# Two rows per partition, result in place, loads and stores in alternate runs: a log-softmax backward kernel on one core

## The chip, the cores and the metric

One core of a Trainium2 chip runs the kernel. The metric is the device time in microseconds (us) of one execution. The span of a profiled execution is about 2 us shorter than the reported time of the same execution. (1925.1 us below is its median when the prediction was made, 1925.3 us that with the result.)

Engines: DVE is VectorE, ACT is ScalarE, SP is SyncE (it issues all transfers here), "SPq" is SP's sequencer. "The engines" without a name are the core's 16 DMA engines, which move the data.

## The reference

```python
batch, seq_len, vocab = 8, 1024, 8192            # 8192 rows of 8192 fp32
def reference(y, dy):
    softmax_x = np.exp(y)
    sum_dy = np.sum(dy, axis=-1, keepdims=True)
    return (dy - softmax_x * sum_dy).astype(np.float32)
```

Two inputs of 268.4 MB are read and one output of 268.4 MB is written: 805.3 MB in all.

## The kernel before

A tile is 128 rows, one row (32 KiB) per partition. Per tile: load dy, load y, reduce dy on DVE, then four times exp on ACT into PSUM and one multiply-add on DVE into a half-row output tile; each finished half row is stored.

```python
    yp = ctx.enter_context(tc.tile_pool(name="yp", bufs=3))
    dyp = ctx.enter_context(tc.tile_pool(name="dyp", bufs=2))
    op = ctx.enter_context(tc.tile_pool(name="op", bufs=2))
    ...
    for i in range(n_tiles):                       # 64 tiles
        ...
        nc.sync.dma_start(out=dy_t[:], in_=dy_f[sl])
        nc.sync.dma_start(out=y_t[:], in_=y_f[sl])
        nc.vector.tensor_reduce(out=s_t[:], in_=dy_t[:], ..., negate=True)
        for h in range(n_half):                    # 2
            o_t = op.tile([P, H], fp32)
            for q in range(n_q):                   # 2
                ...
                nc.scalar.activation(e_t[:], y_t[:, cs], ...Exp)
                nc.vector.scalar_tensor_tensor(out=o_t[...], in0=e_t[:], scalar=s_t[:],
                                               in1=dy_t[:, cs], op0=mult, op1=add)
            nc.sync.dma_start(out=out_f[sl][:, h * H : (h + 1) * H], in_=o_t[:])
```

All transfers are issued by SP in one order, on one queue. That order is not quite the order of the code: the built program has it as dy0, y0, dy1, then for every tile "store, store, next y, next-but-one dy":

```
1 L50 DMACopy dy_t<-in_dy_dram 128x8192
2 L51 DMACopy y_t<-in_y_dram 128x8192
3 L50 DMACopy dy_t<-in_dy_dram 128x8192
4 L78 DMACopy out_dram<-o_t 128x4096 x2
5 L51 DMACopy y_t<-in_y_dram 128x8192
6 L50 DMACopy dy_t<-in_dy_dram 128x8192
7 L78 DMACopy out_dram<-o_t 128x4096 x2
```

## Time and profile before

| | before |
|---|---|
| time, median | 1925.1 us (1923.6 to 1926.8) |
| bytes moved | 805.3 MB at a mean of 418 GB/s |
| DMA engines' packets, share of span | 99.5% |
| DVE / ACT busy | 59% / 25% |

Lines of the page of the kernel before: span and busy time, then the DMA rows of the 40 slices (busy tenths; GB/s), the DMA queue (packets, MB, share of 16 engines), the chain that ended last, and the DMA issues (count, KB each, median us from issue to landing).

```profile
span 1924.6 us, 1253 instructions
DVE 1134.1 (59%) x320; ACT 477.5 (25%) x257; POOL 0.2 (0%) x4
...
DMA  9999999999999999999999999999999999999997
GB/s 414 426 432 415 425 424 420 423 420 423 420 414 425 422 420 423 414 424 420 421 423 414 420 422 421 418 422 422 418 426 420 418 425 425 414 425 414 425 425 318
...
q1 hardware_dynamic: 36864, 805.32, 99.5%
...
DMA y_t<-in_y_dram 61%; DVE o_t L70 29%; ACT e_t L67 6%; SPq L78 1%; DVEq L104 0%; ACTq L67 0%; SPq L51 0%; SPq L50 0%
...
dy_t<-in_dy_dram SPq DMA_DIRECT2D x64, 4096.0 KB, 27.8
y_t<-in_y_dram SPq DMA_DIRECT2D x64, 4096.0 KB, 18.3
out_dram<-o_t SPq DMA_DIRECT2D x128, 2048.0 KB, 8.7
```

One tile in the timeline of the kernel before (start us, length us, engine, line, what, count; in brackets the idle time before and what ended it):

```profile
888.61 3.68 ACT L67 ACTIVATE e_t<-y_t 128x2048 f32<-128x2048 f32 x2 [21.56 <-DMA y_t<-in_y_dram]
890.52 9.12 DVE L70 SCALAR_TENSOR_TENSOR o_t<-e_t,s_t,dy_t 128x2048 f32<-128x2048 f32 x4 [12.28 <-ACT e_t L67]
...
895.16 4.86 SPq L78 DMA_DIRECT2D out_dram<-o_t  x2
...
900.43 0.60 SPq L51 DMA_DIRECT2D y_t<-in_y_dram  x1
901.09 1.23 SPq L50 DMA_DIRECT2D dy_t<-in_dy_dram  x1
918.38 3.68 ACT L67 ACTIVATE e_t<-y_t 128x2048 f32<-128x2048 f32 x2 [21.34 <-DMA y_t<-in_y_dram]
```

### The profile page before, as it was taken

What the parts mean: (1) busy time and instruction counts of PE and PEld (TensorE: products, weight loads), DVE (VectorE), ACT (ScalarE), POOL (GpSimd) and SP (SyncE); (2) the same over time, 40 slices, a digit from 0 to 9 for tenths busy, and PEclk for the clock granted to TensorE, in tenths of its full rate; (3) what the DMA queues carried; (4) which work ended last, traced back from release to release, by engine and by line L of the source; (5) the groups of instructions that cost most, each with busy time, mean ns of one, the idle gap of its engine ahead of it and who ended that gap; (6) DMA issues with size and microseconds to landing.
All of it is one profiled execution on the core that took longest, in us unless ns stands there. A gap on an engine that the chain in (4) does not pass through costs nothing.

```text
span 1924.6 us, 1253 instructions
## 1 busy us (share of the span) xinstructions
DVE 1134.1 (59%) x320; ACT 477.5 (25%) x257; POOL 0.2 (0%) x4
## 2 busy tenths in 40 slices
DVE  5657556465564655756657556475564655646555
ACT  1322313223132131221322313223132231321312
POOL 0000000000000000000000000000000000000000
DMA  9999999999999999999999999999999999999997
GB/s 414 426 432 415 425 424 420 423 420 423 420 414 425 422 420 423 414 424 420 421 423 414 420 422 421 418 422 422 418 426 420 418 425 425 414 425 414 425 425 318
DMA packets 36874, 805.40 MB, mean 418 GB/s; under 512 B 4096, under 2 KB 4096, under 8 KB 4096
## 3 DMA queue, kind: packets, MB, share of 16 engines
q1 hardware_dynamic: 36864, 805.32, 99.5%
q14 instruction: 10, 0.08, 0.0%
HBM read 536.87 MB, written 268.44 MB: 418 GB/s over the span
## 4 chain that ended last, share of the span: by engine, by line
DMA 61%; DVE 29%; ACT 6%; issue 2%; SPq 1%; DVEq 0%; ACTq 0%
DMA y_t<-in_y_dram 61%; DVE o_t L70 29%; ACT e_t L67 6%; SPq L78 1%; DVEq L104 0%; ACTq L67 0%; SPq L51 0%; SPq L50 0%
## 5 line engine op out<-in xcount | busy, mean ns | idle before, releaser
L70 DVE SCALAR_TENSOR_TENSOR o_t<-e_t,s_t,dy_t 128x2048 f32<-128x2048 f32 x256 | 584.1, 2344 | 770.0 <-ACT e_t L67 770.0
L67 ACT ACTIVATE e_t<-y_t 128x2048 f32<-128x2048 f32 x256 | 476.2, 1877 | 1436.2 <-DMA y_t<-in_y_dram 1372.4
L53 DVE TENSOR_REDUCE s_t<-dy_t 128x1 f32<-128x8192 f32 x64 | 555.2, 8676 | 12.9 <-DMA dy_t<-in_dy_dram 12.9
L67 ACT ACT_TABLE_LOAD x1 | 1.3, 1283 | 0.7 <-PEq L93 0.7
L93 POOL MEMSET const-bfloat16-1.0<- 128x1 bf16 x1 | 0.1, 102 | 0.0
L93 POOL MEMSET const-uint8-127<- 128x1 uint8 x1 | 0.1, 102 | 0.0
L93 POOL MEMSET const-float32-0.0<- 128x1 f32 x1 | 0.1, 99 | 0.2 <-issue 0.2
L93 POOL MEMSET const-float32-1.0<- 128x1 f32 x1 | 0.1, 99 | 0.0
## 6 DMA issues: line engine op xcount, KB each, us to landing
dy_t<-in_dy_dram SPq DMA_DIRECT2D x64, 4096.0 KB, 27.8
y_t<-in_y_dram SPq DMA_DIRECT2D x64, 4096.0 KB, 18.3
out_dram<-o_t SPq DMA_DIRECT2D x128, 2048.0 KB, 8.7
```

What stands on the lines that cost most here:

```text
L53: nc.vector.tensor_reduce(out=s_t[:], in_=dy_t[:], axis=mybir.AxisListType.X, op=mybir.AluOpType.add, negate=True,)
L67: nc.scalar.activation(e_t[:], y_t[:, cs], mybir.ActivationFunctionType.Exp)
L70: nc.vector.scalar_tensor_tensor(out=o_t[:, q * CD : (q + 1) * CD], in0=e_t[:], scalar=s_t[:], in1=dy_t[:, cs], op0=mybir.AluOpType.mult, ...
L78: nc.sync.dma_start(out=out_f[sl][:, h * H : (h + 1) * H], in_=o_t[:])
L93: nc = _bacc.Bacc("TRN2", target_bir_lowering=False, num_devices=1)
```

## The change

Intent: longer contiguous runs (two rows per partition as one 64 KiB run for dy and the output), no separate output tile (the result replaces dy), and fewer changes of direction: 32 MB loaded, then 16 MB stored, 16 times, on the one queue.

```diff
-    yp = ctx.enter_context(tc.tile_pool(name="yp", bufs=3))
-    dyp = ctx.enter_context(tc.tile_pool(name="dyp", bufs=2))
-    op = ctx.enter_context(tc.tile_pool(name="op", bufs=2))
+    R = 2
+    BATCH = 2
+    dy_v = dy.flatten_outer_dims().rearrange("(g p r) d -> g p (r d)", p=P, r=R)
     ...
+    dyp = ctx.enter_context(tc.tile_pool(name="dyp", bufs=BATCH))
+    yp = ctx.enter_context(tc.tile_pool(name="yp", bufs=2))
-    for i in range(n_tiles):
     ...
+    for b in range(0, G, BATCH):
+        done = []
+        for g in range(b, b + BATCH):
+            dy_t = dyp.tile([P, R * D], fp32, name="dy_t")
+            nc.sync.dma_start(out=dy_t[:], in_=dy_v[g])
+            for r in range(R):
+                y_t = yp.tile([P, D], fp32, name="y_t")
+                nc.sync.dma_start(out=y_t[:], in_=y_v[g][:, r * D : (r + 1) * D])
     ...            # R reductions, then R times four exp + multiply-add into dy_t
+            done.append((g, dy_t))
+        for g, dy_t in done:
+            nc.sync.dma_start(out=out_v[g], in_=dy_t[:])
```

A batch is two groups of 256 rows; "store0" and "store1" below are its two stores of 8 MB.

More of the change, by code (lines that the diff above doesn't have):

```diff
@@ L8, with subtract_scaled_exp @@
 from concourse.bass import ts
+ACT_EXP = mybir.ActivationFunctionType.Exp
+ALU = mybir.AluOpType
+def subtract_scaled_exp(nc, psum, y_part, dy_part, neg_sum, width):
+    total = y_part.shape[-1]
+    for c in range(0, total, width):
+        e_t = psum.tile([128, width], mybir.dt.float32, name="e_t")
+        nc.scalar.activation(e_t[:], y_part[:, c : c + width], ACT_EXP)
+        nc.vector.scalar_tensor_tensor(
+            out=dy_part[:, c : c + width],
+            in0=e_t[:],
+            scalar=neg_sum,
+            in1=dy_part[:, c : c + width],
+            op0=ALU.mult,
+            op1=ALU.add,
+        )
 @with_exitstack
@@ L21 @@
     fp32 = mybir.dt.float32
-    y_f = y.flatten_outer_dims()
-    dy_f = dy.flatten_outer_dims()
-    out_f = out.flatten_outer_dims()
-    N, D = y_f.shape
-    assert N % P == 0, (N, P)
-    n_tiles = N // P
-    n_half = 2
-    H = D // n_half
-    n_q = 2
-    CD = H // n_q
-    assert CD * 4 * 2 <= 16 * 1024, "psum budget"
-    yp = ctx.enter_context(tc.tile_pool(name="yp", bufs=3))
-    dyp = ctx.enter_context(tc.tile_pool(name="dyp", bufs=2))
-    op = ctx.enter_context(tc.tile_pool(name="op", bufs=2))
+    N, D = y.flatten_outer_dims().shape
@@ L40 @@
+    R = 2
+    G = N // (P * R)
+    assert N == G * P * R
+    BATCH = 2
+    assert G % BATCH == 0
+    CD = 2048
+    y_v = y.flatten_outer_dims().rearrange("(g p r) d -> g p (r d)", p=P, r=R)
+    dy_v = dy.flatten_outer_dims().rearrange("(g p r) d -> g p (r d)", p=P, r=R)
+    out_v = out.flatten_outer_dims().rearrange("(g p r) d -> g p (r d)", p=P, r=R)
+    dyp = ctx.enter_context(tc.tile_pool(name="dyp", bufs=BATCH))
+    yp = ctx.enter_context(tc.tile_pool(name="yp", bufs=2))
     psum = ctx.enter_context(tc.tile_pool(name="psum", bufs=2, space=bass.MemoryType.PSUM))
@@ L41 @@
     stats = ctx.enter_context(tc.tile_pool(name="stats", bufs=8))
-    for i in range(n_tiles):
-        sl = ts(i, P)
-        dy_t = dyp.tile([P, D], fp32)
-        y_t = yp.tile([P, D], fp32)
-        s_t = stats.tile([P, 1], fp32)
-        nc.sync.dma_start(out=dy_t[:], in_=dy_f[sl])
-        nc.sync.dma_start(out=y_t[:], in_=y_f[sl])
-        nc.vector.tensor_reduce(
-            out=s_t[:],
-            in_=dy_t[:],
-            axis=mybir.AxisListType.X,
-            op=mybir.AluOpType.add,
-            negate=True,
-        )
-        for h in range(n_half):
-            o_t = op.tile([P, H], fp32)
-            for q in range(n_q):
-                c = h * n_q + q
-                cs = slice(c * CD, (c + 1) * CD)
-                e_t = psum.tile([P, CD], fp32)
-                nc.scalar.activation(
-                    e_t[:], y_t[:, cs], mybir.ActivationFunctionType.Exp
-                )
-                nc.vector.scalar_tensor_tensor(
-                    out=o_t[:, q * CD : (q + 1) * CD],
-                    in0=e_t[:],
-                    scalar=s_t[:],
-                    in1=dy_t[:, cs],
-                    op0=mybir.AluOpType.mult,
-                    op1=mybir.AluOpType.add,
-                )
-            nc.sync.dma_start(out=out_f[sl][:, h * H : (h + 1) * H], in_=o_t[:])
@@ new lines @@
+    for b in range(0, G, BATCH):
[3 more added lines that the diff above has]
+            nc.sync.dma_start(out=dy_t[:], in_=dy_v[g])
+            y_ts = []
+            for r in range(R):
+                y_t = yp.tile([P, D], fp32, name="y_t")
+                nc.sync.dma_start(out=y_t[:], in_=y_v[g][:, r * D : (r + 1) * D])
+                y_ts.append(y_t)
+            sums = []
+            for r in range(R):
+                s_t = stats.tile([P, 1], fp32, name="s_t")
+                nc.vector.tensor_reduce(
+                    out=s_t[:],
+                    in_=dy_t[:, r * D : (r + 1) * D],
+                    axis=mybir.AxisListType.X,
+                    op=ALU.add,
+                    negate=True,
+                )
+                sums.append(s_t)
+            for r in range(R):
+                subtract_scaled_exp(
+                    nc, psum, y_ts[r], dy_t[:, r * D : (r + 1) * D], sums[r][:], CD
+                )
+            done.append((g, dy_t))
+        for g, dy_t in done:
+            nc.sync.dma_start(out=out_v[g], in_=dy_t[:])
```

## The prediction

> **What bounds it now.** The transfers. The page gives 805.4 MB at a mean of 418 GB/s over 1924.6 us, all on one queue whose packets fill 99.5% of 16 engines' span; DVE is busy 59%, ACT 25%. The chain of waits agrees (61% y_t). The Trainium skill ("DMA: Bandwidth & Descriptors", Where 436 GB/s comes from) gives 435 GB/s as the fabric ceiling; the trace's load stretches come within 1% of it, so only about 70 us (805.3 MB at 435 GB/s is 1851 us) can be won.
>
> **Where those 70 us are**, from the single transfer packets of the trace. A 32 KiB load packet takes 1213 ns (432 GB/s over 16 engines), a 16 KiB store packet 611 to 614 ns (429 GB/s): about 9 ns per packet beyond bytes at 435 GB/s. Undisturbed packets sum to 1868 us. Head and tail: first packet at 1.75 us, about 10 us of idle transfer engines after the last y landed (1904 to 1914, computing the last tile), 1.3 us after the last semaphore; 13 us. The rest, about 43 us, are turnarounds: once per 128-row tile, where stores give way to loads, the last 32 of 256 store packets stretch to 767 and 951 ns (0.51 us over 16 engines); loads lose 0.15 us where stores begin. 0.67 us x 64 tiles = 43 us.
>
> **What the change does.**
> - Turnarounds: 64 pairs become 16 (32 MB in, 16 MB out). 48 x 0.67 = 32 us, if one costs the same after a long store run (assumed).
> - Packets: dy and out in 64 KiB runs, y still 32 KiB. At 9 ns each the sum falls from 1868 to about 1859 us; 9 us. If 64 KiB is split in two, 5 us of it is lost.
> - Tail: the store of the last group's neighbour (8 MB, 19 us) covers the last compute, so the 10 us of idle engines go.
> - Compute keeps count and shapes (64 reductions of 8.68 us, 256 exps and multiply-adds at 2.29 us) and stays hidden.
>
> **Does the queue stay fed?** Order: dy0, y, y, dy1, y, y, store0, store1, next dy0. The tightest wait is store1's: from dy1's last byte, 0.4 us to start, two reductions 17.4, eight multiply-adds 18.3, issue to first packet 1.1: 37.2 us. Meanwhile the engines have y, y and store0: 19.4 + 19.3 = 38.7 us. Slack only 1.5 us, per 48 MB batch. If it is negative by d, the loss is 16 x d. The next dy0 waits for store0's landing; store1's 19 us cover that. The y reloads have over 8 us to spare.
>
> **Sum:** 1859 + 16 x 0.67 + 4 (head, tail) = **1874 us**, 2.7% faster; 1860 to 1897 should hold it 8 times in 10. Chances: faster by over 2% 0.77, within 2% 0.21, slower by over 2% 0.02.
>
> **What would show it.** Packets: about 16384, plus semaphores, of 65536 and 32768 bytes, the large ones near 2417 ns. Stretched store packets at 16 places, not 64, same loss each. Mean rate near 430 GB/s, with the last slices full. SP waiting for DVE before store1, the engines never empty there.
>
> **What would make it wrong.** Store1's slack being negative (gap in the transfer timeline between store0 and store1, up to some 1 us each: 1890 us). Long store runs of 39 us not holding 429 GB/s, since before shows only 10 us runs, or a turnaround that grows with the run. The 64 KiB pitch meeting slower memory access. Engines drifting apart over longer runs.

## More of the kernel before

The granted clock was 1.0 in every run, and executions of one kernel agree within about 0.3%.

The runs come from four sessions on different chips. The kernel before ran in each, with medians of 1925.3 to 1926.6 us, so a difference of 1 or 2 us between runs of different sessions is not shown by their times alone.

## The result

The changed kernel takes **1877.6 us** (median; 1877.4 to 1879.8) against 1925.3 us for the kernel before. The ratio is 0.9753, 95% interval 0.9739 to 0.9767; ratios here are the mean time of one kernel's fast runs over that of the other's of the same rounds, so not quite the ratio of the medians. The prediction was 1874 us with 1860 to 1897, and faster by over 2% was given 0.77.

Lines of the page of the changed kernel, to set against those of before:

```profile
span 1876.0 us, 939 instructions
DVE 1131.1 (60%) x320; ACT 480.3 (26%) x257; POOL 0.2 (0%) x4
...
DMA  9999999999999999999999999999999999999999
GB/s 425 425 425 434 438 425 446 421 432 442 428 426 433 435 428 444 425 423 433 425 440 425 422 429 426 444 425 426 434 437 425 432 429 429 430 432 421 425 436 393
...
q1 hardware_dynamic: 18432, 805.31, 99.9%
...
DMA out_dram<-dy_t 34%; DMA dy_t<-in_dy_dram 32%; DVE dy_t L20 16%; DVE s_t L74 15%; DVEq L114 0%; DVEq L20 0%
...
y_t<-in_y_dram SPq DMA_DIRECT2D x64, 4096.0 KB, 29.0
dy_t<-in_dy_dram SPq DMA_DIRECT2D x32, 48.2
out_dram<-dy_t SPq DMA_DIRECT2D x32, 33.1
```

Everything stands longer in the queue, the last slice is nearly full (393 instead of 318 GB/s: the exposed end is gone), and the mean rate is 429 GB/s. But DVE is still 31% of the chain.

**Where the time went, from the single transfer packets of the trace.** Undisturbed, a 16 KiB packet takes 611 ns, one of 32 KiB 1213 ns, one of 64 KiB 2418 ns. "Packets" is the number of packets times these figures, with the 4-byte completion packets at 9 ns, over 16 engines; "stretch" is what the packets took beyond it; "gaps" are times over 0.1 us in which an engine had no packet, "end" those in the last 25 us. The trace does not name a packet's engine, so for the gaps each packet was joined to the one whose end it follows most closely. Records overlap a little (8.9 us in all before, 4.3 us in the changed kernel), and some 3 us of head and tail come on top, so rows do not add up exactly to the time. The same table for all runs (us, over 16 engines):

```
kernel                              packets  stretch   gaps    end     time
before                               1870.1     44.8    4.0    9.7   1925.3
changed                              1860.2     13.9    1.2    0.0   1877.6
e1: 32 KiB runs, 16 alternations     1864.9      3.9    0.2    0.0   1870.9
e2: 32 KiB runs, 32 alternations     1864.9      4.3    0.2    0.0   1871.4
e3: 32 KiB runs, 64 alternations     1864.9      3.9    0.1    0.0   1871.7
e4: one alternation, no arithmetic   1864.9      5.6    0.0    0.0   1869.9
e5: changed, store1 2.2 us later     1860.2     26.4    6.7    0.0   1893.6
e6: changed, store1 8.7 us later     1860.2     29.1   97.2    6.2   1993.7
e7: before, last tile cut finer      1870.4     44.5    3.5    0.1   1918.9
e8: changed, stores on ACT's queue   1860.2     52.7   10.1   20.0   1942.6
e9: before, y load moved ahead       1870.1      3.1    0.2    6.8   1877.3
e3b: e3 with a shallower queue       1864.9      3.9    0.1    6.3   1874.4
e3c: e3b with 11 us more DVE work    1864.9      4.3    1.2   15.7   1885.7
e10: changed, one row's sum on ACT   1860.2      4.2    0.2    0.0   1868.1
```

From before to changed, stretch falls by 30.9 us, packets by 9.9, the idle end by 9.7, gaps by 2.8. The prediction had 32, 9 and 10. These are 53.3 us; the smaller overlap of the fewer records takes 4.6 us back, which leaves 48.7 against 47.7 measured. So the books close within about 1 us, and with entries like the predicted ones. What remained to test was the cause behind the largest: do packets stretch because the direction changes?

### The profile page after: what moved, and what is told of

The parts are those of the page before. It is cut to its first block, busy times and chain, and to the rows that moved or that the text cites. A ratio compares the mean times of both kernels' runs of the same rounds, so it can differ in the third digit from the quotient of the medians.

```text
span 1876.0 us, 939 instructions
## 1 busy us (share of the span) xinstructions
DVE 1131.1 (60%) x320; ACT 480.3 (26%) x257; POOL 0.2 (0%) x4
## 2 busy tenths in 40 slices
DMA packets 18440, 805.38 MB, mean 429 GB/s; under 512 B 2048, under 2 KB 2048, under 8 KB 2048
## 4 chain that ended last, share of the span: by engine, by line
DMA 66%; DVE 31%; issue 1%; another core or an unknown queue 0%; DVEq 0%
DMA out_dram<-dy_t 34%; DMA dy_t<-in_dy_dram 32%; DVE dy_t L20 16%; DVE s_t L74 15%; DVEq L114 0%; DVEq L20 0%
## 5 line engine op out<-in xcount | busy, mean ns | idle before, releaser
L20 DVE SCALAR_TENSOR_TENSOR dy_t<-e_t,s_t,dy_t 128x2048 f32<-128x2048 f32 x256 | 580.8, 2341 | 0.0
```

Of the source, the lines that this page charges most:

```text
L20: nc.vector.scalar_tensor_tensor(out=dy_part[:, c : c + width], in0=e_t[:], scalar=neg_sum, in1=dy_part[:, c : c + width], op0=ALU.mult, o ...
```

## The experiments

### First round: is it the number of alternations?

Theory 1, the prediction's: each change from stores to loads (and back) costs some 0.67 us; the change takes away 48 of 64. Rivals: the 64 KiB runs bring the gain; or in-place results and the covered end do. e1 to e3 share 32 KiB runs, whole-row stores in place, and a covered end, and differ in how often they alternate; each has its loads queued well ahead of the stores.

**e1_r1_b4**: the changed kernel with one row per partition.

```diff
-    R = 2
+    R = 1
-    BATCH = 2
+    BATCH = 4
```

> One row per partition again (32 KiB runs everywhere), but still 32 MB in, 16 MB out: 16 turnarounds, result in place. Theory (turnarounds bring most of the gain, long runs little): 24576 packets of 1213 ns over 16 engines are 1863 us against 1859 us of the changed kernel, so it should be some 4 us slower than the changed kernel's 1877.6 us: 1880 to 1883 us. Rival (the 64 KiB runs bring the gain): most of the 48 us is lost again, 1900 us or more.

Measured: 1870.9 us, ratio to before 0.9715 (0.9701 to 0.9728). Not 4 us slower than the changed kernel but about 7 us faster, without the 64 KiB runs. Both theories missed.

**e2_r1_b2**: the loop rewritten for 16 MB in, 8 MB out (four dy tiles, in place).

```diff
+    load(0)
+    load(1)
+    for t in range(0, G, 2):
+        compute(t)
+        if t + 2 < G:
+            load(t + 2)
+        compute(t + 1)
+        if t + 3 < G:
+            load(t + 3)
+        store(t)
+        store(t + 1)
```

> As the run with 32 KiB runs and 16 turnarounds, but 16 MB in, 8 MB out: 32 turnarounds. Theory: 16 more turnarounds at 0.65 to 0.75 us each, 10 to 12 us more than that run, 1891 to 1894 us. Rival one (long runs): same as that run. Rival two (the gain is from the result in place, so whole-tile stores and a covered last compute, not from the alternation): same as that run.

Measured: 1871.4 us, ratio 0.9718 (0.9705 to 0.9731). Theory 1 expected 20 us more.

**e3_r1_b1**: the same for 8 MB in, 4 MB out.

```diff
+    for t in range(G):
+        compute(t)
+        if t + 2 < G:
+            load(t + 2)
+        store(t)
```

> As before, with 8 MB in, 4 MB out: 64 turnarounds, as many as the kernel before has, but in place, whole-tile stores of 32 KiB runs and the last compute mostly covered. Theory: 48 more turnarounds than with 16, 31 to 36 us more, 1911 to 1918 us; its distance to the kernel before (some 10 us) is then packets (6 us) and tail. Rival two (in place and covered tail are the gain): 1880 us.

Measured: 1871.7 us, ratio 0.9720 (0.9707 to 0.9733), with 3.9 us of stretch. As many alternations as the kernel before, and no cost: from 16 to 64 alternations the time rises by 0.8 us. **Theory 1 falls.**

**e4_one_turn**: all loads, then all stores, no arithmetic (a wrong result).

```diff
+    for t in range(G):
+        dy_t = dyp.tile([P, D], fp32, name="dy_t")
+        nc.sync.dma_start(out=dy_t[:], in_=dy_v[t])
+        y_t = yp.tile([P, D], fp32, name="y_t")
+        nc.sync.dma_start(out=y_t[:], in_=y_v[t])
+    for t in range(G):
+        nc.sync.dma_start(out=out_v[t], in_=dy_t[:])
```

> Wrong result on purpose: all 128 loads of 4 MB, then all 64 stores, 32 KiB runs, no arithmetic; one turnaround. Theory: 1863 us of packets + 4 us head and tail + 1 us: 1868 us of span, 1869 to 1871 us. If long store runs cannot hold the rate of short ones, it is slower than the run with 16 turnarounds.

Measured: 1869.9 us, as expected. It bounds what alternating can cost at all with 32 KiB runs: e3, with 64 alternations and all the arithmetic, is only 1.8 us above it.

### The end of the kernel, and the slack of store1

**e7_tail**: the kernel before, with the last tile's y loaded and its result stored in quarters.

```diff
+        n_p = n_half * n_q if i == n_tiles - 1 else 1
+        for c in range(n_p):
+            w = slice(c * (D // n_p), (c + 1) * (D // n_p))
+            nc.sync.dma_start(out=y_t[:, w], in_=y_f[sl][:, w])
     ...
+                if i == n_tiles - 1:
+                    nc.sync.dma_start(out=out_f[sl][:, cs], in_=o_t[:, q * CD : (q + 1) * CD])
```

> The kernel before with the last tile only cut finer: y loaded in four DMAs, the result stored in four DMAs. Theory (about 10 us of idle transfer engines at the end of the kernel before): three quarters of that compute are covered, 6 to 7 us faster than before: 1918 to 1919 us. Rival (the tail is covered already): same as before.

Measured: 1918.9 us, ratio 0.9972 (0.9958 to 0.9986): the expected size. The idle end of the kernel before is a real cost, 6.9 us of its 9.7 can be had there alone, and stretch stays at 44.5 us.

**e5_slack2** and **e6_slack8**: the changed kernel with a needless reduction of 2048 (e6: 8192) columns in the second group of each batch, so that store1 is ready later. The result is unchanged.

```diff
+            if g == b + BATCH - 1:
+                x_t = stats.tile([P, 1], fp32, name="x_t")
+                nc.vector.tensor_reduce(out=x_t[:], in_=dy_t[:, 0:2048],   # e6: 0:8192
+                                        axis=mybir.AxisListType.X, op=ALU.add)
```

> The changed kernel with one needless reduction of 2048 columns (about 2.2 us on DVE) in the second group of each batch only; result unchanged. Theory (store1 is ready only 1.5 us before the engines would run dry): the slack turns into a gap of about 0.7 us, 16 times: some 11 us slower than the changed kernel, 1888 us. Rival (compute is hidden, DVE is busy 60%): no change, 1877 us.

> The same with a needless reduction of 8192 columns (8.68 us) in the second group of each batch. Theory: 8.7 - 1.5 = 7.2 us of empty engines in each of 16 batches, about 115 us slower: 1992 us. Rival (hidden compute): 1877 us.

Measured: e5 1893.6 us (ratio 0.9839, 0.9826 to 0.9853), e6 1993.7 us (1.0358, 1.0344 to 1.0372). For e5 1888 us were expected. "Hidden compute" is refuted: with DVE busy some 60% of the time, 2.2 us of it per batch cost 16 us in 16 batches. The second group of e6 in the timeline:

```profile
1052.40 48.58 SPq L96 DMA_DIRECT2D out_dram<-dy_t  x2
1056.49 17.28 DVE L74 TENSOR_REDUCE s_t<-dy_t 128x1 f32<-128x8192 f32 x2 [4.11 <-DMA dy_t<-in_dy_dram]
...
1073.68 8.68 DVE L84 TENSOR_REDUCE x_t<-dy_t 128x1 f32<-128x8192 f32 x1
1082.45 18.16 DVE L20 SCALAR_TENSOR_TENSOR dy_t<-e_t,s_t,dy_t 128x2048 f32<-128x2048 f32 x8
```

From the landing of dy at 1056.5 runs an unbroken DVE chain to 1100.6, and only then is the second store issued (the pair of issues covers 1052.40 to 1100.98). The total of e6 agrees with the expectation, but its parts do not: gaps are 103 us of it (97.2 and 6.2; 6.5 per batch, not 7.2), and 15 us are additional stretch, which nobody expected. In e5 gaps account for 5.5 us more and **stretch for 12.5 us more** than in the changed kernel. So lateness of a store brings stretch, beyond the gap itself. That gave the second theory.

**e8_two_queues**: the changed kernel with its stores issued from ACT's queue.

```diff
-            nc.sync.dma_start(out=out_v[g], in_=dy_t[:])
+            nc.scalar.dma_start(out=out_v[g], in_=dy_t[:])
```

> The changed kernel with the stores issued from ACT's queue, so that the next batch's dy may enter the engines beside store1. If a turnaround costs because the engines change direction, mixing packets of both directions for some 39 us of each batch costs many changes and is slower than 1877.6 us by tens of us. If it costs only because a queue must drain at the change, mixing hides it and up to 10 us are won: 1868 us.

Measured: 1942.6 us, ratio 1.0093 (1.0079 to 1.0107), so 65 us slower than the changed kernel. The DMA queues of e8 (packets, MB, share of 16 engines):

```profile
q1 hardware_dynamic: 13824, 536.88, 65.5%
q10 hardware_dynamic: 4608, 268.44, 33.0%
```

Loads and stores really ran on two queues, and packets stretched by 52.7 us; another 20 us are an idle end. Taken alone, the expectation would read this as a cost of changing direction. After e3 that does not hold for one queue; e8 shows that mixing both directions from two queues is costly, not why. It is inconclusive for the main question, and a warning for its own.

### Second theory: the store that comes just in time

Theory 2: packets stretch where a store reaches the engines only when they are about to finish what they have; a store queued some microseconds earlier costs nothing, however often the direction changes.

It can be tested inside a single trace. Take as margin of a store the mean time of the 16 completion packets of the transfer ahead of it, minus the store's issue, minus 1.05 us (about the delay at the start of the kernel: issue at 0.73, first data packet at 1.75). The 15 full batches of the changed kernel, with store1's margin and the stretch in that batch's two changes of direction that follow (us):

```
batch     0    1    2    3    4    5    6    7    8    9   10   11   12   13   14
margin 2.41 1.55 1.66 0.97 1.30 0.54 0.90 0.86 0.47 1.28 0.69 1.62 0.49 1.30 -0.63
stretch 0.02 0.18 0.11 0.47 0.23 1.12 1.12 1.11 1.51 0.65 1.23 0.07 1.34 0.43 1.61
```

The correlation is -0.89. In the kernel before, margin of the first store of a tile (median 0.31 us) against stretch at the next change: -0.90 over 63 tiles. Same change of direction, same kernel, and the cost runs from nothing to 1.6 us with the time in hand. In the kernel before 119 of 127 stores have a margin under 1 us; in the changed kernel 8 of 31, all of them store1. In e1 to e3, which showed no cost of alternating, the median margins are 26, 36 and 43.5 us.

A correlation is no cause, so the margin was moved on purpose, from both sides.

**e9_y_ahead**: the kernel before, with the next tile's loads written ahead of this tile's stores. In the built order dy of the next tile already stood there, so only y moves. Nothing else: 16 KiB store runs, two stores per tile, the separate output tile and 64 alternations stay.

```diff
+    ahead = load(0)
     for i in range(n_tiles):
         sl = ts(i, P)
-        dy_t = dyp.tile([P, D], fp32)
-        y_t = yp.tile([P, D], fp32)
+        dy_t, y_t = ahead
+        if i + 1 < n_tiles:
+            ahead = load(i + 1)
         s_t = stats.tile([P, 1], fp32)
-        nc.sync.dma_start(out=dy_t[:], in_=dy_f[sl])
-        nc.sync.dma_start(out=y_t[:], in_=y_f[sl])
```

> The kernel before with one thing moved: the next tile's y load is issued ahead of this tile's stores instead of behind them; 16 KiB store runs, two stores per tile, 64 alternations and the last tile's exposed compute stay. New theory (a change of direction costs only where the stores come just as the engines run dry, which sets the engines going anew each time): the stores now are queued some 12 us early, the stretched packets (42 us) vanish, 1882 to 1888 us. Rival A (64 changes of direction cost): 1925 us. Rival B (store packets of another size than the load packets reshuffle the engines at each change): 1915 us or more.

Measured: **1877.3 us**, ratio 0.9742 (0.9728 to 0.9757). The interval overlaps that of the whole change (0.9739 to 0.9767): one load moved ahead in the queue brings as much as the change does. Stretch falls from 44.8 to 3.1 us. It is even some 5 us under the expected range, in part because the end was 6.8 us idle, not 10, and because the gaps went too (4.0 to 0.2 us). Rivals A (count of alternations) and B (packets of different size) fall here, and so does the first round's rival of the result in place: the separate output tile is still there. The chain and the landing times of e9:

```profile
DMA out_dram<-o_t 82%; DVE o_t L75 16%; DMA y_t<-in_y_dram 1%; DVEq L75 0%; DVEq L109 0%; ACT e_t L72 0%; SPq L46 0%
...
out_dram<-o_t SPq DMA_DIRECT2D x128, 2048.0 KB, 24.4
```

and one tile in its timeline:

```profile
891.04 3.68 ACT L72 ACTIVATE e_t<-y_t 128x2048 f32<-128x2048 f32 x2 [17.79 <-DMA y_t<-in_y_dram]
896.06 9.34 DVE L75 SCALAR_TENSOR_TENSOR o_t<-e_t,s_t,dy_t 128x2048 f32<-128x2048 f32 x4 [6.07 <-DMA out_dram<-o_t]
...
900.70 5.08 SPq L83 DMA_DIRECT2D out_dram<-o_t  x2
...
905.83 0.42 SPq L46 DMA_DIRECT2D dy_t<-in_dy_dram  x1
906.34 0.38 SPq L47 DMA_DIRECT2D y_t<-in_y_dram  x1
```

A store now stands 24.4 us between issue and landing instead of 8.7, DVE now waits for landed stores that free the output tile (394.7 us in all on the page of e9, none before), and the chain's share of compute has gone from 35% to 16%.

**e3b_shallow**: e3 with the store behind one tile of loads instead of two.

```diff
         compute(t)
+        store(t)
         if t + 2 < G:
             load(t + 2)
-        store(t)
```

> The run with 8 MB in, 4 MB out, with each tile's store queued behind one tile of loads instead of two, so some 8 us before it is needed; uniform 32 KiB runs. New theory (only running dry matters): as that run, 1871 to 1873 us. Rival C (the new direction must be queued over 25 us ahead): stretched packets return, 1895 us or more.

Measured: 1874.4 us, ratio 0.9729 (0.9715 to 0.9744), 1 us over the expected range, stretch 3.9 us; the 3 us over e3 come with a 6.3 us idle end. Stores now have a median margin of 13.4 us instead of 43.5, and it makes no difference: rival C falls.

**e3c_dry**: e3b with needless reductions of 8192 and 2048 columns per tile.

```diff
+        for c in (8192, 2048):
+            x_t = stats.tile([P, 1], fp32, name="x_t")
+            nc.vector.tensor_reduce(out=x_t[:], in_=dy_ts[t][:, 0:c], axis=mybir.AxisListType.X, op=ALU.add)
```

> The same with needless reductions of 8192 and 2048 columns per tile, so that each store comes about 1 us too late, 64 times; result unchanged. New theory: gaps of about 1.2 us x 64 = 77 us and, beyond them, stretched packets of 0.6 to 0.8 us per tile, 40 to 50 us: 1985 to 2000 us, with over 30 us of stretch in the packets. Rival B (only mixed packet sizes reshuffle the engines): gaps alone, 1950 us, and stretch under 5 us.

Measured: 1885.7 us, ratio 0.9788 (0.9771 to 0.9804), stretch 4.3 us, gaps 1.2 us. The experiment failed to make its condition: I had left out that the store of the tile ahead (9.7 us) also runs in the meantime, so the stores still had a median margin of 5.2 us. It therefore says nothing on rival B. It does say that DVE at 97% busy does no harm as long as the stores are some microseconds early; most of the 11 us over e3b are its end, idle 9.4 us longer.

**e10_act_sum**: the changed kernel with one of four row sums per batch moved from DVE to ACT, so that store1 is ready earlier. Packets, alternations and order stay.

```diff
-            for r in range(R):
+            n_dve = R if g == b else R - 1
+            for r in range(n_dve):
                 s_t = stats.tile([P, 1], fp32, name="s_t")
     ...
+            if n_dve < R:
+                p_t = stats.tile([P, D // CD], fp32, name="p_t")
+                for c in range(D // CD):
+                    j_t = psum.tile([P, CD], fp32, name="e_t")
+                    nc.scalar.activation(j_t[:], dy_t[:, D + c * CD : D + (c + 1) * CD],
+                                         ...Identity, accum_out=p_t[:, c : c + 1])
+                s_t = stats.tile([P, 1], fp32, name="s_t")
+                nc.vector.tensor_reduce(out=s_t[:], in_=p_t[:], ..., op=ALU.add, negate=True)
```

> The changed kernel, 64 KiB runs kept, with the sum of the second row of each batch's second group moved from DVE to ACT, so that store1 is ready some 10 us before the engines need it instead of about 2. Result correct. New theory: the stretched packets vanish and the lower packet sum of 64 KiB runs shows: 1859 us of packets + 3 head and tail + 1 to 2, 1865 to 1868 us, the fastest of all. Rival B (64 KiB beside 32 KiB packets): still 1877 us.

Measured: **1868.1 us**, correct, ratio 0.9697 (0.9682 to 0.9711): the lowest median of all, and faster than both kernels. (Its lead of 2.8 us over e1 is not shown by the times: they ran in different sessions, and their intervals overlap.) Stretch falls from 13.9 to 4.2 us. Store1's median margin is 4.7 us (at least 3.3; some 10 were expected), against 1.1 in the changed kernel, -0.3 in e5 and -6.5 in e6. The second group in its timeline:

```profile
877.03 8.69 DVE L76 TENSOR_REDUCE s_t<-dy_t 128x1 f32<-128x8192 f32 x1 [3.44 <-DMA dy_t<-in_dy_dram]
...
888.72 9.13 DVE L20 SCALAR_TENSOR_TENSOR dy_t<-e_t,s_t,dy_t 128x2048 f32<-128x2048 f32 x4 [2.94 <-ACT e_t L19]
...
898.42 9.13 DVE L20 SCALAR_TENSOR_TENSOR dy_t<-e_t,s_t,dy_t 128x2048 f32<-128x2048 f32 x4 [0.58 <-ACT e_t L19]
```

and that of the changed kernel, in two cuts of its timeline:

```profile
879.02 17.28 DVE L74 TENSOR_REDUCE s_t<-dy_t 128x1 f32<-128x8192 f32 x2 [3.42 <-DMA dy_t<-in_dy_dram]
...
896.22 18.15 DVE L20 SCALAR_TENSOR_TENSOR dy_t<-e_t,s_t,dy_t 128x2048 f32<-128x2048 f32 x8
...
914.40 0.34 SPq L88 DMA_DIRECT2D out_dram<-dy_t  x1
918.69 0.34 SPq L65 DMA_DIRECT2D dy_t<-in_dy_dram  x1
```

From dy's landing to the last multiply-add it takes 35.3 us in the changed kernel and 30.5 us in e10 (898.42 + 9.13 - 877.03), where DVE now waits a little for y. Some 5 us of compute in each of 16 batches, off the busiest resource by every summary, are worth 9.5 us of the kernel in all. Set against e5 and e6, store1's margin was moved by DVE or ACT work alone from -6.5 over -0.3 and 1.1 to 4.7 us, and stretch went 29.1, 26.4, 13.9, 4.2: a dose and its response.

The rates over 1600 us of the middle, from the windows of before, changed and e10 (stretch from to, its length, busy time of DVE, ACT and POOL with counts, clock, DMA share, GB/s):

```profile
200.00:1800.00 1600.00, 951.31 (x270) 401.83 (x216) 0.00 (x0) 1.00 1.00 421
```

```profile
200.00:1800.00 1600.00, 955.73 (x272) 405.26 (x217) 0.00 (x0) 1.00 1.00 431
```

```profile
200.00:1800.00 1600.00, 850.20 (x272) 506.51 (x322) 0.00 (x0) 1.00 1.00 433
```

The DMA share is 1.00 in all three. Only the rate tells them apart, and only the length of single packets tells why.

**What stays open.** A late store has its effect not at once but at the changes of direction that follow: in e6 the restart at store1 stretches packets by only 0.08 us, and each of the two changes after it by about 0.8. Why that is so, no run here settles. In the kernels without stretch, the order in which the 16 engines finish a transfer, as far as it can be reconstructed, mostly stays the same from one transfer to the next, and in before and changed it is shuffled more often; this may be part of the cause or another effect.

## Why the prediction was right or wrong

- **The time and the verdict were right**: 1874 predicted, 1877.6 measured, 2.5% faster where 2.7% was foreseen. In its largest term this was luck, as the next point shows.
- **"only about 70 us ... can be won"**: an estimate, worked out from the 435 GB/s that the prediction cites. No run contradicts it; e10 won 58.5 us (1926.6 to 1868.1 us in its session).
- **"Turnarounds: 64 pairs become 16 ... 32 us, if one costs the same after a long store run (assumed)"**: this step failed: the size was right (stretch fell by 30.9 us), the cause was wrong. The number of turnarounds is worth about 1 us between 16 and 64 (e1, e3). What the change took away were just-in-time stores: of 119 stores with a margin under 1 us, 8 were left. That the loss per pair came out alike (0.75 us, the mean of the 15 batches above, against the 0.67 assumed) is luck: single batches range from 0.02 to 1.6 us, so the prediction's own check, "same loss each", failed. The prediction saw that stretch sits at the changes of direction, and took the place for the cause; all turnarounds it had seen were of stores that came late, so its trace could not tell the two apart.
- **"Packets ... 9 us"**: measured 9.9 us, 1.2 of it completion packets; but 4.6 us of that went back into the smaller overlap of records, so about 5 us of time are left, and the term was too large. As a cause by itself: e10 against e1 (64 against 32 KiB for dy and output, neither with much stretch) differ by 2.8 us of time and 4.7 us of packets, but in different sessions.
- **"Tail: ... the 10 us of idle engines go"**: measured 9.7 us, and e7 had 6.9 us of it alone.
- **"Slack only 1.5 us"**: measured median margin 1.1 us; the estimate was good. But its consequence was misjudged: a small positive slack was held to be free, and only a negative one to cost its gap. In fact the thin slack is what the changed kernel loses most by, 9.5 us against e10.
- **"Compute ... stays hidden"**: it did not; DVE is 31% of the chain after the change, and e10 shows what that costs.
- In-place results and whole-row stores cost nothing that the runs show; DVE's multiply-add took 2341 ns after and 2344 ns before.

## What to carry to other kernels

Where DMA engines look 100% busy, compare the length of single packets with that of undisturbed ones: packets can stretch, and the share of busy time hides it. Look up how long a store takes from issue to landing; if it is hardly longer than its own transfer, the queue is running on what has just been computed, and issuing the next loads ahead of the store (or shortening the compute chain ahead of it) can be worth more than longer runs and fewer alternations. A right total does not prove its parts: here a term of the right size had the wrong cause, and only kernels that kept the alternations and moved the issue showed it.

## What the Trainium skill lacked or had wrong

- "DMA: Bandwidth & Descriptors", Where 436 GB/s comes from: the fabric ceiling of 435 GB/s agrees with the runs (433 GB/s over 1600 us in e10). The same section says that the HBM side, about 358 GB/s, binds for transfers between HBM and SBUF; for one core these runs do not agree, with a mean of 431 GB/s over the whole of e10. "HBM Reference", Specifications (TRN2), has about 425 GB/s for a core streaming alone, which is closer.
- No page we read has that a store issued just in time stretches packets at the next changes of direction: 44.8 us of 1925 in the kernel before, 3.1 us once the y load was issued ahead of it. The advice in "DMA: Bandwidth & Descriptors", Rules for kernel authors, to issue a DMA early names only the fixed setup cost.
- The same section says that spreading transfers over several issuing engines does not help bandwidth. Here it did harm: stores on ACT's queue beside loads on SP's made the changed kernel 65 us slower (1877.6 to 1942.6 us), 20 us of it an idle end.
- The same page, Latency and other measured facts, gives about 600 ns to the first byte for this kind of issue, and does not say from where it counts. Here the first data packet started 1.02 us after the start of the issuing instruction (0.73 to 1.75 us) and 0.63 us after its end (1.12 us), so only the count from the end agrees.
- No page we read has the cost of alternating between loads and stores on one queue: about 0.8 us of 1871 between 16 and 64 alternations (e1, e3), if the stores are queued early.
